# A two-layer decoder trunk on one core: slots ordered by the end of their last use, MLP activations stored in two steps, down operands gated by their loads

## The chip, the cores and the metric

The kernel runs on one core of one Trainium2 chip. The metric is the device time of one execution in microseconds; the figure for a kernel is the median of its runs. All arithmetic is on float32 values.

## What is computed

Two layers, each `h += post_norm(mixer(pre_norm(h)))` and then `h += post_norm(mlp(pre_norm(h)))`, on 1024 tokens by 1024 features. The mixers differ (gated MLP and pooling in layer 0, differential attention and a short convolution in layer 1). The change touches the MLP alone, which is the same in both layers:

```python
def squared_relu_mlp(h, w1, w2):                 # w1: 1024 x 4096, w2: 4096 x 1024
    return jnp.square(jax.nn.relu(h @ w1)) @ w2
```

## The kernel before

**Precision.** Every float32 operand is split in two parts: ScalarE casts a high part (`split_slot`, L624) and VectorE subtracts it for the low part (L625). A product is then three matmuls (`mm3`, L237 to L239: high by high, and the two cross terms).

**Tiling.** Each MLP matrix product is done by a 2 x 2 block scheme with seven products in place of eight. In the up half (`mlp_up`, L745) the 4096 hidden features go in 16 chunks `q`; a chunk has seven products of 12 matmuls (`plain` makes two, then `p6`, `p5`, `p7`, `p4`, `p3`). The first six chunks (`EARLY`) have done their two plain products ahead, so their iterations have five products. ScalarE copies partial sums out of PSUM (L753) and squares (L756, L757); VectorE forms sums of weights (`w1_sums`, L663 to L666) and of results. `sums(q)` (L824) forms the operands of the down half and issues four stores on the POOL queue: three pairs `x0`, `x1`, `x2` of 512 KB each (L838) and a half slot `u` of 256 KB (L839), all to the DRAM array `hs`. Eight units of the planner's clock later the four slots go back to the free list (L840).

The down half (`Down`, L1266) reads `hs` and `w2` again. Its 28 operand pairs are taken in the order of `ORDER`, four groups of seven. A product `n` is four quarters of 12 matmuls; the first four kinds of each group add up in the PSUM banks `pA`, the others in `pC`, and ScalarE copies the bank after each quarter in the first group (L1424), VectorE adds it to `acc` in the later ones (L1426). `prep(n)` takes the slots for product `n`, issues the load of the next activations (`load_h(n + 1)`) and some loads of weights on the SP queue (L614), and returns a list of steps: the two casts and subtractions of the activations (`hh`, `hl` from `hr`) first, then those of the weights (`wh`, `wl` from `w2r` or from a sum `t`). `step` runs the steps: two per quarter, or as many as are needed. It may begin `prep(n + 2)` while product `n` runs (`AHEAD = 2`), if 14 slots are free.

**Slots.** All of this lives in 50 slots of 4 KB per partition (`Slots`, L31). The free list is first in, first out. The planner's clock (`k.clock`) advances by the cost of each product (`pe`, 12 x 0.227 for a quarter or an up product) and says when `later` work is due. The order in the text is a priority: the framework then orders each engine's instructions by when it expects their operands, so an instruction can be put ahead of text that comes before it, and on the chip an engine runs its own list strictly in that order. A slot that is handed out again makes its new writer wait for all readers of the old content, a store among them.

Of the kernel before, what the change touches and what calls it, by code (L numbers as in the profile page):

```python
# [16 lines left out]
ALU = mybir.AluOpType  # L17
# [13 lines left out]
class Slots:  # L31


    def __init__(self, pool, n):
        self.pool = pool
        self.free = list(range(n))
        self.n = 0
        self.low = n
        self.live = {}

    def get(self, shape, dtype, name):
        if not self.free:
            raise RuntimeError(f"out of SBUF slots at {name}: {sorted(self.live.values())}")
        i = self.free.pop(0)
        self.low = min(self.low, len(self.free))
        self.n += 1
        self.live[i] = name
        t = self.pool.tile(shape, dtype, tag=f"s{i}", name=f"{name}_{self.n}")
        return Slot(self, i, t)


class Slot:
    def __init__(self, owner, i, t):
        self.owner, self.i, self.t = owner, i, t

    def put(self):
        self.owner.free.append(self.i)
        del self.owner.live[self.i]
        self.t = None


# [88 lines left out]
class Trunk:  # L150
    def __init__(self, ctx, tc, a):
        self.tc, self.nc, self.a = tc, tc.nc, a
        self.clock = 0.0
        self.q = []
        self.seq = 0
        self.small = ctx.enter_context(tc.tile_pool(name="small", bufs=1))
        self.tiny = ctx.enter_context(tc.tile_pool(name="tiny", bufs=5))
        self.slots = Slots(ctx.enter_context(tc.tile_pool(name="slots", bufs=1)), NSLOT)
        self.psp = ctx.enter_context(tc.tile_pool(name="psp", bufs=1, space=bass.MemoryType.PSUM))
        self.banks = list(range(8))  # L160
        dram = ctx.enter_context(tc.tile_pool(name="dram", bufs=1, space=bass.MemoryType.DRAM))
        self.hd = [dram.tile([S, DM], F32, name=f"hd{i}") for i in range(3)]
        self.ydd = dram.tile([2, 2, P, S], F32, name="ydd")
        self.skew = dram.tile([4, P * 384], F32, name="skew")
        self.W = Weights(self)
        self.ydone = {}
        self.xn = [[[None] * 4 for _ in range(2)] for _ in range(2)]
        self.xready = [[False, False], [False, False]]
        self.pend = {}
        self.xr = {}  # L170
        self.hs = [dram.tile([7, 4, P, 2048], F32, name=f"hs{i}") for i in range(2)]
# [573 lines left out]
    def mlp_up(self, layer):  # L745
        nc, sl = self.nc, self.slots
# [3 lines left out]
        Q = [dict() for _ in range(NQ)]  # L750
# [4 lines left out]
        def relu2(ap, src):  # L755
            nc.scalar.activation(ap, src, AF.Relu)  # L756
            nc.scalar.activation(ap, ap, AF.Square)  # L757
# [49 lines left out]
        def p4(q):  # L807
            d = Q[q]
            self.prod1(d["A"], q, "x", 0, "t4", False)
            self.w1q[q]["x"].put()  # L810
            relu2(d["x0"].t[:, 1, :], d["A"].t)
            d["A"].put()

        def p3(q):
            d = Q[q]
            self.prod1(d["C"], q, "sb", 1, "b22", False)
            for n in ("sb", "hsb"):
                self.w1q[q][n].put()
            c12 = d["x1"].t[:, 0, :]
            tt(c12, d["C"].t, d["u"].t[:, 1, :], op=ALU.add)  # L820
            d["C"].put()
            relu2(c12, c12)

        def sums(q):  # L824

            d = Q[q]
            g, r = q // 4, slice((q % 4) * 512, (q % 4) * 512 + 512)
            a11, a12 = d["x0"].t[:, 0, :], d["x0"].t[:, 1, :]
            a21, a22 = d["x1"].t[:, 0, :], d["x1"].t[:, 1, :]
            d["x2"] = sl.get([P, 2, 512], F32, "hx2")  # L830
            s1, s2 = d["x2"].t[:, 0, :], d["x2"].t[:, 1, :]
            tt(s1, a21, a22, op=ALU.add)
            tt(s2, s1, a11, op=ALU.subtract)
            tt(a21, a11, a21, op=ALU.subtract)
            tt(d["u"].t[:, 1, :], a12, s2, op=ALU.subtract)
            hs = self.hs[layer]
            for n, j in (("x0", 0), ("x1", 2), ("x2", 4)):
                nc.gpsimd.dma_start(hs[j:j + 2, g, :, r].rearrange("j p f -> p j f"), d[n].t)  # L838
            nc.gpsimd.dma_start(hs[6, g, :, r], d["u"].t[:, 1, :])  # L839
            self.later(8.0, lambda: [d[n].put() for n in ("x0", "x1", "x2", "u")])  # L840


        self.wait(lambda: self.xready[0] == [True, True])
# [30 lines left out]
        down = None  # L874
        for q in range(NQ):
            n = q + 1
            if n < NQ:
                if n > 1:
                    self.w1_sums(n)
                if n >= EARLY:  # L880
                    plain(n)
                if n > 1:
                    self.w1_split(n, "b")
                if n < EARLY:
                    p6(n)
                if self.HELD <= n + 1 < EARLY:
                    refill(n + 1)
                if q == 0:
                    next(xs)
            else:  # L890
                down.step(4, 0)
            p4(q)
            if n < NQ:
                self.w1_split(n, "a")
                if q == 0:
                    next(xs)
            else:
                down.step(8, 0)
            p3(q)
            if n < NQ:  # L900
                if n >= EARLY:
                    p6(n)
                if n + 2 < NQ:
                    if "raw" not in self.w1q[n + 2]:
                        self.w1q[n + 2]["raw"] = self.raw_w1(layer, n + 2)
                self.w1_a22(n)
                p5(n)
                sums(q)
                if n + 1 < NQ and n + 1 >= EARLY:
                    self.w1_plain(n + 1)  # L910
                p7(n)
                if n == NQ - 2:
                    down = Down(self, layer)
                    down.load_w(0, 11)
                    down.load_h(0)
                if n == NQ - 1:
                    down.load_h(1)
                    down.load_w(0, 22)
                    down.load_w(0, 12)
            else:  # L920
                sums(q)
# [344 lines left out]
class Down:  # L1266
# [10 lines left out]
    def __init__(self, k, layer):  # L1277
        self.k, self.layer = k, layer
        self.seq = [(g, i) for g in range(4) for i in self.ORDER]
        self.H, self.Wd, self.B, self.T = {}, {}, {}, {}  # L1280
        self.acc, self.banks = {}, {}
        self.todo = []
        self.ready = 0
        self.begun = 0

    def pair(self, name, dt=F32R):
        return [self.k.slots.get([P, 2, 512], dt, name) for _ in range(2)]

    def load_h(self, n):
        if n >= len(self.seq) or n in self.H:  # L1290
            return
        g, i = self.seq[n]
        self.H[n] = self.pair("hr", F32)
        for j in range(2):
            self.k.load(self.H[n][j].t.rearrange("p a b -> p (a b)"),
                        self.k.hs[self.layer][self.HJ[i], g, :, j * 1024:j * 1024 + 1024])

    def load_w(self, g, kn):

        if g > 3:  # L1300
            return
        self.B[g, kn] = self.pair("w2r", F32)
        b = (kn // 10 - 1) * 2 + kn % 10 - 1
        for j in range(2):
            self.k.load(self.B[g, kn][j].t.rearrange("p a b -> p (a b)"),
                        self.k.a["w2"][self.layer, g, b, :, j * 1024:j * 1024 + 1024])
# [19 lines left out]
    def prep(self, n):  # L1326
# [2 lines left out]
        T, B = self.T, self.B  # L1329
        hl = [self.pair("hh"), self.pair("hl")]  # L1330
        wl = [self.pair("wh"), self.pair("wl")]
        steps = self.split(hl, self.H.pop(n))
        self.load_h(n + 1)
        if i == 1:
            steps += self.split(wl, B[g, 11], True)
            T[3] = self.pair("t3", F32)
            steps += self.sub(T[3], B[g, 22], B[g, 12])
        elif i == 6:
            self.load_w(g, 21)
            T[2] = self.pair("t2", F32)  # L1340
            steps = self.tt(T[2], T[3], B[g, 11], ALU.add) + steps
            steps += self.split(wl, T[2], True)
        elif i == 7:
            steps += self.split(wl, T.pop(3))
# [12 lines left out]
            steps += self.split(wl, B.pop((g, 22 if i == 3 else 21)))  # L1357
            self.load_w(g + 1, 22 if i == 3 else 12)
        self.Wd[n] = (*hl, *wl)
        steps.append(self.one_ready)  # L1360
        return steps

    def one_ready(self):
        self.ready += 1

    AHEAD = 2

    def step(self, n, most):

        while n > 0:  # L1370
            if not self.todo:
                if (self.begun >= len(self.seq) or self.begun > most
                        or (self.begun > most - self.AHEAD + 1 and len(self.k.slots.free) < 14)):
                    return
                self.todo = self.prep(self.begun)
                self.begun += 1
            self.todo.pop(0)()
            n -= 1

    def finish(self, m):  # L1380
        while self.ready <= m:
            self.step(1, m)

    def run(self, hsrc, hdst):
        k, acc, seq = self.k, self.acc, self.seq
# [165 lines left out]
```

## Time and profile before

| | us |
|---|---|
| median of 3 runs | 1991.13 |
| lowest, highest run | 1985.10, 1991.89 |
| the profiled execution, its own time | 1989.53 |
| span from its first to its last instruction | 1987.7 |

TensorE (PE) is busy for nearly the whole span, so the time can only fall by the stretches in which PE waits or runs at a lower clock. In the tables of the trace "idle before" is the time an engine stood still ahead of an instruction, and the name behind the arrow is what ended it; `DMA hs<-hx` is the landing of a store of `x0`, `x1` or `x2`, `DMA hs<-u` that of `u`, `DMA hr<-hs` that of a load of activations.

### The profile page before, as it was taken

How to read it: one execution, taken by the hardware profiler on the slowest of the kernel's cores; microseconds unless marked ns; L12 is line 12 of the kernel's file. 1: busy time of each engine (PE TensorE's matmuls, PEld its weight loads, DVE VectorE, ACT ScalarE, POOL GpSimd, SP SyncE). 2: the span in 40 equal slices, each digit the busy share in tenths (PEclk: the TensorE clock that was granted, in tenths of full speed). 3: DMA queues.
4: the chain of work that ended last, by engine and by line, in shares of the span. 5: the costliest groups of instructions: out<-in, count | busy, mean ns of one | idle time of the engine just before them, and what ended most of it. 6: DMA issues, size and time to landing. Idle time of an engine off the chain costs nothing.

```text
span 1987.7 us, 23663 instructions
## 1 busy us (share of the span) xinstructions
PE 1948.4 (98%) x8840; PEld 1588.7 (80%) x8840; DVE 1278.4 (64%) x1979; ACT 982.9 (49%) x1632; POOL 208.5 (10%) x327
## 2 busy tenths in 40 slices
PE   9999999999999999999999999999999999999997
PEld 6888887788877888878778778788777888788886
DVE  5664496655577777683455556658665657767776
ACT  7223574555455443474344444657545545544342
POOL 3101101111110000031000001120111111000001
PEclk9999999999999999999999999999999999999999
DMA  8114226755675534452111103323565557544453
GB/s 296 42 61 131 85 97 189 181 148 148 181 211 183 176 108 161 161 187 82 43 43 43 32 33 106 117 96 106 162 185 151 154 160 226 181 146 160 150 177 130
DMA packets 77011, 269.84 MB, mean 136 GB/s; under 512 B 9221, under 2 KB 9221, under 8 KB 76896
## 3 DMA queue, kind: packets, MB, share of 16 engines
q1 hardware_dynamic: 48816, 170.94, 25.8%
q0 software_dynamic: 26784, 95.26, 16.4%
q10 hardware_dynamic: 1296, 2.13, 0.3%
q8 instruction: 69, 1.13, 0.2%
q14 instruction: 46, 0.38, 0.1%
HBM read 189.92 MB, written 78.38 MB: 135 GB/s over the span
## 4 chain that ended last, share of the span: by engine, by line
PE 59%; issue 29%; POOL 4%; DMA 3%; DVE 3%; ACT 1%; SPq 0%; POOLq 0%; DVEq 0%; ACTq 0%
PE pA L237 5%; PE pA L238 5%; PE pA L239 5%; PE pC L237 4%; PE pC L238 4%; PE pC L239 4%; POOL hs L838 3%; PE op L237 3%; PE op L239 3%; PE op L238 3%; PE pv L1226 1%; PE s L1159 1%; DMA hr<-hs 1%; DMA hs<-hx 1%; PE s L1162 1%
## 5 line engine op out<-in xcount | busy, mean ns | idle before, releaser
L624 ACT CAST hh<-hr 128x1024 fp32r<-128x1024 f32 x112 | 117.8, 1054 | 200.5 <-DMA hr<-hs 159.4
L237 PE MATMUL pA<-wh,hh 128*128 128x512 f32 x512 | 200.7, 392 | 8.0 <-ACT acc L1424 8.0
L238 PE MATMUL pA<-wl,hh 128*128 128x512 f32 x512 | 200.1, 391 | 0.8 <-DVE wl L625 0.8
L239 PE MATMUL pA<-wh,hl 128*128 128x512 f32 x512 | 200.0, 391 | 0.0
L625 DVE TENSOR_TENSOR hl<-hr,hh 128x1024 fp32r<-128x1024 f32 x112 | 136.2, 1222 | 89.9 <-ACT hh L624 86.7
L237 PE MATMUL pC<-wh,hh 128*128 128x512 f32 x384 | 150.1, 391 | 0.8 <-DVE acc L1426 0.8
L238 PE MATMUL pC<-wl,hh 128*128 128x512 f32 x384 | 149.7, 390 | 0.0
L239 PE MATMUL pC<-wh,hl 128*128 128x512 f32 x384 | 149.5, 389 | 0.0
L838 POOL DMA_DIRECT2D hs<-hx x96 | 69.3, 723 | 557.8 <-ACT hx L757 408.1
L237 PEld LDWEIGHTS pA<-wh,hh 128*128 128x128 f32 x512 | 96.5, 188 | 31.3 <-ACT acc L1424 11.0
L238 PEld LDWEIGHTS pA<-wl,hh 128*128 128x128 f32 x512 | 96.5, 188 | 21.4 <-DVE wl L625 1.4
L239 PEld LDWEIGHTS pA<-wh,hl 128*128 128x128 f32 x512 | 96.4, 188 | 19.9
L756 ACT ACTIVATE hx<-hx 128x512 f32<-128x512 f32 x96 | 60.7, 632 | 100.3 <-DVE hx L775 45.8
L114 DVE TENSOR_TENSOR wlo<-raw,whi 128x1024 fp32r<-128x1024 f32 (+1 forms) x57 | 68.3, 1203 | 48.4 <-ACT whi L113 31.1
L1426 DVE TENSOR_TENSOR acc<-acc,pA 128x512 f32<-128x512 f32 x96 | 65.2, 683 | 36.5 <-PE pA L239 36.5
L1195 ACT ACTIVATE e<-s,nm 128x512 f32<-128x512 f32 (+3 forms) x96 | 54.6, 579 | 63.7 <-DVE nm L1188 54.0
L237 PEld LDWEIGHTS pC<-wh,hh 128*128 128x128 f32 x384 | 72.3, 188 | 16.4 <-DVE acc L1426 1.2
L113 ACT CAST whi<-raw 128x1024 fp32r<-128x1024 f32 (+1 forms) x57 | 58.8, 1041 | 52.8 <-PE pp L239 15.8
L238 PEld LDWEIGHTS pC<-wl,hh 128*128 128x128 f32 x384 | 72.2, 188 | 14.9
L239 PEld LDWEIGHTS pC<-wh,hl 128*128 128x128 f32 x384 | 72.2, 188 | 14.9
L757 ACT ACTIVATE hx<-hx 128x512 f32<-128x512 f32 x128 | 81.1, 633 | 3.4
L625 DVE TENSOR_TENSOR wl<-w2r,wh 128x1024 fp32r<-128x1024 f32 x64 | 76.9, 1221 | 7.8 <-ACT wh L624 3.6
(332 smaller groups left out, 5156.3 us busy)
## 6 DMA issues: line engine op xcount, KB each, us to landing
hr<-hs SPq DMA_DIRECT2D x112, 512.0 KB, 5.3
hs<-hx POOLq DMA_DIRECT2D x96, 512.0 KB, 5.0
w1r<-in_w_dram SPq DMA_DIRECT2D x74, 512.0 KB, 4.3
w2r<-in_w_dram SPq DMA_DIRECT2D x64, 512.0 KB, 8.0
h<-hd POOLq DMA_DIRECT2D x24, 512.0 KB, 5.4
hs<-u POOLq DMA_DIRECT2D x32, 256.0 KB, 7.6
hd<-y POOLq DMA_DIRECT2D x12, 512.0 KB, 3.0
rx<-in_xT_dram SPq DMA_DIRECT2D x16, 256.0 KB, 7.4
```

The lines of the kernel that those rows point to most:

```text
L113: k.nc.scalar.copy(u.hi.t[:, f], u.raw.t[:, f])
L114: k.nc.vector.tensor_tensor(u.lo.t[:, f], u.raw.t[:, f], u.hi.t[:, f].bitcast(F32), op=ALU.subtract)
L237: mm(ps, ah, bh, start=start, stop=False, skip_group_check=more)
L238: mm(ps, ah, bl, start=False, stop=False, skip_group_check=more)
L239: mm(ps, al, bh, start=False, stop=stop, skip_group_check=more)
L624: self.nc.scalar.copy(hi, src)
L625: self.nc.vector.tensor_tensor(lo, src, hi.bitcast(F32), op=ALU.subtract)
L756: nc.scalar.activation(ap, src, AF.Relu)
L757: nc.scalar.activation(ap, ap, AF.Square)
L838: nc.gpsimd.dma_start(hs[j:j + 2, g, :, r].rearrange("j p f -> p j f"), d[n].t)
L1195: nc.scalar.activation(e[m][:, kb * 512:kb * 512 + n], banks[m, kb][:, :n], AF.Exp, scale=SCALE, bias=nm[:, m:m + 1], accum_out=sm[:, kb * ...
L1426: nc.vector.tensor_tensor(o, o, bank.t, op=ALU.add)
```

## The change

1. A slot that is put back carries a time, the planner's clock plus `after`; `get` takes the free slot with the lowest one. `after` is 6.0 for `x1`, `x2` and `u` at the end of `sums`, and 0 everywhere else.
2. The store of `x0` is issued at the end of `p4` and no longer in `sums`; the other three stay.
3. In `prep` the steps on the activations come last, behind those on the weights.
4. `step` begins the look-ahead `prep(n + 2)` only if at least 8.0 units of the planner's clock have gone by since the last load of the down half was issued.
5. In the last iteration of the up half the two calls `down.step(4, 0)` and `down.step(8, 0)` become `down.step(5, 1)` twice; `finish` calls `step` with a limit one higher.

```diff
     def get(self, shape, dtype, name):
-        i = self.free.pop(0)
+        i = min(self.free, key=lambda j: self.cool[j])
+        self.free.remove(i)
...
-    def put(self):
-        self.owner.free.append(self.i)
-        del self.owner.live[self.i]
+    def put(self, after=0.0):
+        o = self.owner
+        o.free.append(self.i)
+        o.cool[self.i] = o.k.clock + after
+        del o.live[self.i]
...
         def p4(q):
             relu2(d["x0"].t[:, 1, :], d["A"].t)
             d["A"].put()
+            store(q, 0, "x0")
...
+        def store(q, j, n):
+            r = slice((q % 4) * 512, (q % 4) * 512 + 512)
+            nc.gpsimd.dma_start(self.hs[layer][j:j + 2, q // 4, :, r].rearrange("j p f -> p j f"), Q[q][n].t)
...
-            for n, j in (("x0", 0), ("x1", 2), ("x2", 4)):
-                nc.gpsimd.dma_start(hs[j:j + 2, g, :, r].rearrange("j p f -> p j f"), d[n].t)
-            nc.gpsimd.dma_start(hs[6, g, :, r], d["u"].t[:, 1, :])
-            self.later(8.0, lambda: [d[n].put() for n in ("x0", "x1", "x2", "u")])
+            store(q, 2, "x1")
+            store(q, 4, "x2")
+            nc.gpsimd.dma_start(self.hs[layer][6, g, :, r], d["u"].t[:, 1, :])
+            self.later(8.0, lambda: [d[n].put(0.0 if n == "x0" else 6.0) for n in ("x0", "x1", "x2", "u")])
...
-                down.step(4, 0)
+                down.step(5, 1)
             p4(q)
...
-                down.step(8, 0)
+                down.step(5, 1)
             p3(q)
...
     def load_h(self, n):
         self.H[n] = self.pair("hr", F32)
+        self.loaded = self.k.clock
...
         self.B[g, kn] = self.pair("w2r", F32)
+        self.loaded = self.k.clock
...
-        steps = self.split(hl, self.H.pop(n))
+        steps, late = [], self.split(hl, self.H.pop(n))
         self.load_h(n + 1)
         if i == 1:
             steps += self.split(wl, B[g, 11], True)
+            steps, late = steps + late, []
...
-            steps = self.tt(T[2], T[3], B[g, 11], ALU.add) + steps
+            steps += self.tt(T[2], T[3], B[g, 11], ALU.add)
...
-        steps.append(self.one_ready)
-        return steps
+        return steps + late + [self.one_ready]
...
-    AHEAD = 2
+    AHEAD, LAND = 2, 8.0
...
                 if (self.begun >= len(self.seq) or self.begun > most
-                        or (self.begun > most - self.AHEAD + 1 and len(self.k.slots.free) < 14)):
+                        or (self.begun > most - self.AHEAD + 1
+                            and (len(self.k.slots.free) < 14 or self.k.clock - self.loaded < self.LAND))):
...
     def finish(self, m):
         while self.ready <= m:
-            self.step(1, m)
+            self.step(1, m + self.AHEAD - 1)
```

## Rows read from the trace of the kernel before

**Rows 1.** The page, busy time of each engine over the span, its share and its instructions.
```profile
PE 1948.4 (98%) x8840; PEld 1588.7 (80%) x8840; DVE 1278.4 (64%) x1979; ACT 982.9 (49%) x1632; POOL 208.5 (10%) x327
```

**Rows 2.** Busy time by stretch: up half of layer 0, start of its down half, the same two of layer 1. Columns: stretch and its length, then us busy and instructions of PE, PEld, DVE, ACT, POOL; granted clock of PE, share of the DMA engines' time, GB/s.
```profile
303.00:560.00 257.00, 252.63 (x1102) 207.12 (x1101) 156.24 (x209) 135.50 (x202) 38.25 (x56) 0.99 0.65 171
560.00:605.00 45.00, 38.60 (x163) 29.72 (x163) 32.16 (x33) 25.68 (x34) 4.75 (x7) 1.00 0.77 210
...
1360.00:1660.00 300.00, 294.75 (x1302) 242.18 (x1301) 193.68 (x250) 165.26 (x247) 39.46 (x58) 1.00 0.52 158
1660.00:1705.00 45.00, 41.84 (x173) 33.01 (x173) 34.15 (x35) 29.22 (x38) 4.75 (x7) 0.96 0.69 210
```

**Rows 3.** What PE waited for in the up half of layer 0 (303 to 560 us): us in total, times, longest.
```profile
PE pA L237 <- ACT u L753: 2.4, 2, 2.2
PE pA L239 <- DVE w1sb L625: 1.6, 1, 1.6
```

**Rows 4.** The same at the start of the down half of layer 0 (560 to 605 us).
```profile
PE pA L237 <- ACT acc L1424: 4.9, 4, 2.2
PE pC L237 <- DVE hx L804: 0.8, 1, 0.8
PE pA L238 <- DVE wl L625: 0.8, 1, 0.8
```

**Rows 5.** The same in the up half of layer 1 (1360 to 1660 us).
```profile
PE pA L237 <- ACT u L753: 3.5, 3, 1.8
PE pA L239 <- DVE w1sb L625: 1.3, 1, 1.3
```

**Rows 6.** The same at the start of the down half of layer 1 (1660 to 1705 us).
```profile
PE pA L237 <- ACT acc L1424: 3.2, 3, 2.0
```

**Rows 7.** The timeline of PE at five of these waits and one matmul behind the first: start, duration, instruction, and in brackets the idle time before it and what ended it.
```profile
339.18 0.50 PE L239 MATMUL pA<-xb,w1sb 128*128 128x512 f32 x1 [1.61 <-DVE w1sb L625]
339.52 0.39 PE L237 MATMUL pA<-xb,w1hsb 128*128 128x512 f32 x1
384.71 0.65 PE L237 MATMUL pA<-xb,w1hsa 128*128 128x512 f32 x1 [2.16 <-ACT u L753]
...
601.40 0.50 PE L237 MATMUL pA<-wh,hh 128*128 128x512 f32 x1 [2.16 <-ACT acc L1424]
...
1494.90 0.50 PE L237 MATMUL pA<-xb,w1x 128*128 128x512 f32 x1 [1.49 <-ACT u L753]
...
1697.88 0.50 PE L237 MATMUL pA<-wh,hh 128*128 128x512 f32 x1 [2.04 <-ACT acc L1424]
```

**Rows 8.** The timeline of DVE and ACT in the up half, instructions that waited for a store.
```profile
332.11 0.69 DVE L663 TENSOR_TENSOR w1va<-w1r 128x512 f32<-128x512 f32 x1 [5.26 <-DMA hs<-u]
...
377.14 1.23 DVE L625 TENSOR_TENSOR w1l<-w1r,w1h 128x1024 fp32r<-128x1024 f32 x1 [4.20 <-DMA hs<-u]
...
1432.67 0.69 DVE L663 TENSOR_TENSOR w1va<-w1r 128x512 f32<-128x512 f32 x1 [4.95 <-DMA hs<-u]
...
1477.38 1.22 DVE L625 TENSOR_TENSOR w1l<-w1r,w1h 128x1024 fp32r<-128x1024 f32 x1 [4.03 <-DMA hs<-u]
...
1492.37 1.05 ACT L624 CAST w1h<-w1r 128x1024 fp32r<-128x1024 f32 x1 [5.29 <-DMA hs<-hx]
```

**Rows 9.** Busy time by stretch, as in group 2, around the two stretches in which PE's clock was lower.
```profile
384.85:388.30 3.45, 3.45 (x9) 2.68 (x10) 1.73 (x3) 0.62 (x1) 2.02 (x3) 0.51 0.74 213
388.30:392.00 3.70, 3.70 (x18) 3.05 (x17) 1.79 (x2) 2.48 (x3) 0.00 (x0) 1.00 1.00 173
...
1699.00:1702.40 3.40, 3.40 (x10) 2.62 (x9) 1.39 (x2) 3.40 (x5) 0.00 (x0) 0.50 0.04 13
```

**Rows 10.** The timeline of ACT and POOL around one iteration of the up half: the last square of `x0`, the store of `x0`, the store of `u`.
```profile
330.07 0.63 ACT L757 ACTIVATE hx<-hx 128x512 f32<-128x512 f32 x1
331.00 0.71 POOL L838 DMA_DIRECT2D hs<-hx  x1 [6.67 <-ACT hx L757]
...
338.53 0.57 POOL L839 DMA_DIRECT2D hs<-u  x1
```

**Rows 11.** All DMAs that write or read `hs`, from issue to landing.
```profile
DMA to landing us min/median/max: 3.5/5.9/11.3
```

**Rows 12.** The timeline of ACT at the start of the down half of layer 0.
```profile
573.54 1.05 ACT L624 CAST wh<-t 128x1024 fp32r<-128x1024 f32 x1 [4.97 <-DMA hs<-u]
...
589.25 1.06 ACT L624 CAST hh<-hr 128x1024 fp32r<-128x1024 f32 x1 [6.74 <-DMA hr<-hs]
...
597.93 2.00 ACT L624 CAST hh<-hr 128x1024 fp32r<-128x1024 f32 x2 [1.75 <-DMA hr<-hs]
...
600.77 0.58 ACT L1424 COPY acc<-pA 128x512 f32<-128x512 f32 x1
...
621.26 1.05 ACT L624 CAST hh<-hr 128x1024 fp32r<-128x1024 f32 x1 [1.65 <-DMA hr<-hs]
```

**Rows 13.** The chain of work that ended last, at the same place: start, us, what.
```profile
583.01 10.03 DMA hs<-hx
593.05 4.79 DMA hr<-hs
```

**Rows 14.** One group of instructions on the tile `acc`: duration min/median/max, first and last start.
```profile
L1424 ACT COPY acc<-pC x24: 569/580/592, 645.9 to 1903.4; 128x512 f32<-128x512 f32 x24
```

**Rows 15.** Who waited for whom over the whole span: us in total, times, longest.
```profile
ACT hh L624 <- DMA hr<-hs: 159.4, 68, 13.4
DVE w1sb L625 <- PE pA L239: 33.7, 16, 3.6
```

**Rows 16.** DMA issues on the SP queue: count, size of one, median us from issue to landing.
```profile
hr<-hs SPq DMA_DIRECT2D x112, 512.0 KB, 5.3
w2r<-in_w_dram SPq DMA_DIRECT2D x64, 512.0 KB, 8.0
```

More of the change, by code (lines that the diff above doesn't have):

```diff
@@ L36, in __init__ @@
         self.free = list(range(n))
+        self.cool = [0.0] * n
+        self.k = None
         self.n = 0
@@ L158, in __init__ @@
         self.slots = Slots(ctx.enter_context(tc.tile_pool(name="slots", bufs=1)), NSLOT)
+        self.slots.k = self
         self.psp = ctx.enter_context(tc.tile_pool(name="psp", bufs=1, space=bass.MemoryType.PSUM))
@@ L835, in sums @@
             tt(d["u"].t[:, 1, :], a12, s2, op=ALU.subtract)
-            hs = self.hs[layer]
-            for n, j in (("x0", 0), ("x1", 2), ("x2", 4)):
-                nc.gpsimd.dma_start(hs[j:j + 2, g, :, r].rearrange("j p f -> p j f"), d[n].t)
-            nc.gpsimd.dma_start(hs[6, g, :, r], d["u"].t[:, 1, :])
-            self.later(8.0, lambda: [d[n].put() for n in ("x0", "x1", "x2", "u")])
+            store(q, 2, "x1")
+            store(q, 4, "x2")
+            nc.gpsimd.dma_start(self.hs[layer][6, g, :, r], d["u"].t[:, 1, :])
+            self.later(8.0, lambda: [d[n].put(0.0 if n == "x0" else 6.0) for n in ("x0", "x1", "x2", "u")])
         self.wait(lambda: self.xready[0] == [True, True])
@@ L1284, in __init__ @@
         self.begun = 0
+        self.loaded = 0.0
     def pair(self, name, dt=F32R):
```

## The prediction

> **What bounds the kernel now.** The page's busy times come first: PE works for 98% of the span, DVE for 64%, ACT for 49% [rows 1]. No change off PE can gain more than what PE loses to waits and to a lower clock. So the next view is busy time by stretch: in the four stretches of the MLPs that the change touches, PE stands still for 4.4, 6.4, 5.3 and 3.2 us (length less busy time) [rows 2]. The waits of PE in the same stretches say on whom. In both up halves it is ACT's copy of a partial sum and DVE's low part of the weights, 2.4 + 1.6 + 3.5 + 1.3 = 8.8 us in seven waits [rows 3, 5]; at both starts of the down half it is nearly always ACT's copy of the bank, 4.9 + 0.8 + 0.8 + 3.2 = 9.7 us in nine [rows 4, 6].
>
> The timeline says why ACT and DVE were late. In the up half the same engine had stood still some us earlier, ahead of an instruction whose slot still held data of a store in flight: DVE 5.26 us before w1va at 332, 4.20 before w1l at 377, ACT 5.29 before w1h at 1492 [rows 8]. About 7 us later PE stops at 339.18 and 384.71, and 2.5 us later at 1494.90 [rows 7]. At the start of the down half ACT stands 4.97 us for a store and 6.74 us for a load of activations [rows 12], and the chain shows where that load was held: a store landed after 10.03 us and only then the load ran, 4.79 us [rows 13]. The reader is to see that a store that lands late in a slot handed out early is what stops PE, two steps removed.
>
> Each stop costs more than its idle time. The step from matmul to matmul is 0.227 us (the code's own cost per matmul); a wait is counted from the modelled end, 0.39 us after the start, and the first step behind it takes 0.34 [rows 7]: 0.16 + 0.11 = 0.27 us on top. Two stops, of 2.16 and 2.04 us, were followed by 3.4 us at the granted clock 0.5, the 1.2 GHz level: 9 matmuls in 3.45 us, where the next stretch has 18 in 3.70 [rows 9], so 1.6 us lost each time.
>
> **The change, part by part.**
>
> Part 1, the order of slots. With `after` zero the lowest time is the slot put back first, as before; so all of it is that x1, x2 and u count as put back 6 units later. I stepped the free list through the code. From chunk 6 on, before, the chunk's hx2, w1h0 and w1l0 take the slots of x1, x2 and u, put back 10.9 units ago. With 6 units taken off they stand at 4.9 and fall behind w1x and w1va (8.2) and one w1sb (5.4), whose last reader is a PE product or a VectorE subtraction that is over. In the short iterations only two to seven slots are free; there w1va(4), which took u, takes a raw weight slot. So the five long waits of [rows 8] should go, with the stops behind them: of 8.8 us all but 0.4 (two of the short ACT waits), 8.4; five times 0.27, 1.4; one stretch at the lower clock, 1.6. **Up half: 11.4 us.**
>
> Is 6 units enough? A slot of q is then preferred from 14 units after `sums`. The stores are issued right behind `sums`, the last of them at 338.53 in the iteration shown, and land 3.5 to 11.3 us after their issue, median 5.9 [rows 10, 11]: 14 covers all. The Trainium skill (DMA: Bandwidth & Descriptors, Anatomy of one DMA) fits 2.0 us plus bytes over 436 GB/s for a DMA from this queue, an estimate of 3.2 us for 512 KB. By it the stores would land ahead of every reuse and this term would be nil; the trace's median is nearly twice that, and the measured waits decide.
>
> Part 2, the store of x0. POOL runs its list in order, and nothing stands between p4 and `sums` on it: the store of x0 is already issued as soon as the last square ends (330.07 + 0.63, issue at 331.00) [rows 10]. Four stores before, four after, the same waits: zero. What hides it is POOL's idleness; no more than the 0.3 us between square and issue can move.
>
> Part 3, activations last, and part 4, the gate. A load of activations is issued by the prep before the one that casts it. Two quarters of a product are 5.45 units, three are 8.17, so a gate of 8.0 makes a look-ahead prep start three quarters behind the last load and not two. Stepping `step` through both halves, this moves eight preps per layer (3, 6, 10, 13, 17, 20, 24, 27) by one quarter, 2.7 us; the reorder moves their casts by up to four steps, two quarters. Together the cast comes 2.7 to 8.2 us later, where ACT waits 159.4 / 68 = 2.3 us on average, 13.4 at most [rows 15]. Behind the cast on ACT stand the copies of the bank that PE waits for: that is the gain, and it counts only in the first group of a layer, where ACT empties the banks. With part 1 the load of activations for the fourth product takes x0's slot and a slot of the first product, no longer x1's, so it need not wait for the 10.03 us store. I count the largest stop of each layer, 2.16 + 2.04, two times 0.27 and the second stretch at the lower clock, 1.6: **start of the down half, 6.3 us.** The rest there, 5.5 us in seven waits and 1.9 for their restarts, 7.4 us, I leave as it is: ACT's 4.97 us at 573 [rows 12] is the cast of a product two ahead into u's slot, and since the reorder also puts the activation slots back later, my list gives that cast the same slot again. Bounds of this part: 0 and 13.7.
>
> What is queued behind the new waits: a prep that is held back delays its loads on SP and its casts on ACT and DVE. Cover: in layer 0 the cast at 621.26 is for a product whose first bank copy is at 645.9 [rows 12, 14], so some 20 us ahead of need.
>
> Part 5, the step budgets. The first prep has seven steps; 12 were allowed, now 10. The second is shut off as before, since the last loads are 0 and 2.7 units old at the two calls and 8 are asked. Zero. In `finish` the higher limit only keeps the gate from blocking a product that is due.
>
> New waits: slots that come later in the list are replaced by slots that PE has just let go, and a new order of the lists can put some instruction badly. The trace has no such wait in this place; the nearest row is DVE waiting for PE's reads, 33.7 / 16 = 2.1 us [rows 15]. Bounds: nothing, or four short iterations in two layers at 2.1, 16.8 us. I take two stops, one per layer, of about 2.1 plus restart: **4.5 us.**
>
> Sum: 11.4 + 6.3 - 4.5 = 13.2 us off the profiled execution's 1989.5 (its span is 1987.7), 1976.3. The median of the runs is 1.6 above the profiled one, so 1978 is the number to compare.
>
> **The rivals.**
>
> *The wait moves to PE's slots.* Writers of the short iterations now get slots released by the product just running, and PE stops for its own weights. For: few free slots there, and such waits exist. Against: most of them are 10 us ahead of use. At the upper bound 17.7 - 16.8 = 0.9 us remain: 1990.
>
> *Earlier loads collide with the last stores.* At the start of the down half the DMA engines are already 0.77 busy [rows 2], and a w2 load lands in 8.0 us where activations take 5.3 [rows 16]. If loads that start earlier lengthen the stores, the 6.3 is lost: 11.4 - 4.5 = 6.9, 1984. The Trainium skill (DMA: Bandwidth & Descriptors, Issuing engines are not separate DMA queues) says that all queues share the same 16 engines and interleave; no row here separates them.
>
> *All stops go.* 12.3 up (with the two small waits), 6.3 and 7.4 down: 26 us, 1965.
>
> *Slower: the gate eats the cover.* Place: the eight held preps of a layer; price a quarter, 2.7 us, each; it decides where a held prep's activations are cast after its product is due, that is when 8.2 us later is more than the lead. The lead of some 20 us speaks against it. If it decided in one layer: 6.9 - 21.8, that is 14.9 us slower, 2006.
>
> *The change does nothing,* because the framework's own ordering undoes it: 1991.
>
> **How the numbers follow.** My forecast 0.46, its own range 1973 to 1984 (charge of 0, half the up gain). Slots of PE 0.20, collision 0.12, all stops gone 0.12, slower 0.06, nothing 0.04. A measurement can tell about 0.5%, 10 us: below 1981 is faster, above 2001 slower. Faster: 0.36 of my forecast, 0.12 of all gone, 0.04 of the collision: 0.52. Slower: 0.06. Same: 0.42. The range reaches from 1966, beside the case of all stops gone, to 1990, which takes in collision and PE's slots.
>
> **What would show it.** Right: no DVE or ACT wait over 2 us on `hs<-u` or `hs<-hx` in the up half, no half-clock stretch near 385 and 1699, ACT's wait for `hr<-hs` well under 159 us, PE idle in the up halves under 2 us each. Part 2 is right if POOL's store of x0 still starts within 0.5 us of the square's end. Wrong: PE waits of the same length with another releaser (PE itself, or SP's loads), or PE's stops in the down half spread over all four groups, which would be the gate.

## The result and the profile after

| | before | after |
|---|---|---|
| median, us | 1991.51 (1985.10 to 1992.30, 4 runs) | 1970.49 (1969.81 to 1972.75, 4 runs) |
| the profiled execution: its time, its span, us | 1989.53, 1987.7 | 1972.75, 1970.8 |

The ratio is 0.9903, 95% interval 0.9881 to 0.9926: about 20 us off, where 13 were forecast. The two profiled executions differ by 16.9 us in span, and that is what can be read stage by stage.

PE's busy time fell by 5.6 us [rows 1]:

```profile
PE 1942.8 (99%) x8840; PEld 1587.9 (81%) x8840; DVE 1279.9 (65%) x1979; ACT 980.7 (50%) x1632; POOL 206.1 (10%) x327
```

The stages are cut at the same instructions in both kernels: at PE's first matmul with `w1hsb`, its last of the up half and its last of the down half, in each layer. So the lengths can be subtracted. Busy time by stretch, columns as in [rows 2]; the kernel before, then after:

```profile
285.91:568.50 282.59, 277.44 (x1210) 227.16 (x1208) 176.13 (x231) 150.78 (x224) 41.03 (x60) 0.99 0.62 164
568.50:887.77 319.27, 310.70 (x1370) 255.26 (x1369) 236.00 (x264) 159.18 (x207) 18.10 (x28) 0.99 0.50 168
1386.86:1667.90 281.04, 275.79 (x1210) 226.02 (x1208) 175.70 (x230) 149.94 (x223) 41.03 (x60) 1.00 0.55 166
1667.90:1976.88 308.98, 305.82 (x1339) 251.69 (x1337) 225.98 (x247) 140.97 (x175) 11.37 (x19) 0.99 0.49 163
```

```profile
284.80:566.01 281.21, 276.84 (x1210) 227.43 (x1208) 175.83 (x231) 149.53 (x224) 40.92 (x60) 0.99 0.64 166
566.01:875.97 309.96, 307.67 (x1370) 253.98 (x1369) 237.17 (x264) 160.01 (x207) 17.53 (x28) 1.00 0.51 172
1375.40:1657.19 281.79, 277.38 (x1210) 227.33 (x1209) 175.34 (x230) 148.94 (x224) 40.91 (x60) 0.99 0.55 167
1657.19:1960.24 303.05, 303.05 (x1339) 250.94 (x1337) 227.35 (x247) 141.08 (x175) 11.31 (x19) 1.00 0.50 165
```

The down halves give 9.3 and 5.9 us, 15.2 in all. The up halves, from which 11.4 was expected, give 1.4 and -0.8, 0.6 in all. A second profile of the changed kernel (below, under the runs that share a chip) has 281.2 and 279.6 us for them, without the stretch at the lower clock that the first has in layer 1: 2.9 us. So the up halves gave between 0.6 and 2.9 us, and the down halves are the same in both profiles within 0.4. What PE waited for in the up half of layer 0 (303 to 560 us), the start of its down half (560 to 605) and the up half of layer 1 (1340 to 1645); at the start of layer 1's down half it waited for nothing [rows 3 to 6]:

```profile
PE pC L245 <- DVE w1sa L631: 1.9, 1, 1.9
PE pA L243 <- ACT u L759: 1.8, 2, 1.6
PE pA L243 <- ACT w1h L630: 0.7, 1, 0.7
...
PE pA L243 <- ACT acc L1438: 1.5, 1, 1.5
...
PE pC L245 <- DVE w1sa L631: 1.8, 1, 1.8
PE pA L243 <- ACT u L759: 1.7, 2, 1.4
PE pA L243 <- ACT w1h L630: 0.7, 1, 0.7
PE pA L245 <- DVE w1sb L631: 0.2, 1, 0.2
```

The up halves have 8.8 us of PE's waits now, 5.1 of them under other names (`w1sa`, `w1h`). Before they had 10.4: the 8.8 of [rows 3, 5], two of 0.4 for `w1sa` that those rows leave out, and the 0.8 for `hx` in [rows 4], which lies at 565.87, before the up half's end. The starts of the down halves had 8.9 without that one, and have 1.5. Lines of after are 6 to 14 higher: the casts are L630, the subtraction of the low part L631, the copies of partial sums L759, of the bank L1438, the first sum of weights L669.

**Where the up half's waits went.** All waits of DVE and ACT for a store of the up half of layer 0 (285.9 to 568.5 us before, 284.8 to 566 after):

```profile
ACT w1h L624 <- DMA hs<-hx: 18.8, 7, 2.9
DVE w1l L625 <- DMA hs<-u: 10.3, 8, 4.2
ACT hh L624 <- DMA hs<-hx: 6.9, 1, 6.9
DVE w1va L663 <- DMA hs<-u: 5.3, 1, 5.3
DVE w1l L625 <- DMA hs<-hx: 4.0, 1, 4.0
ACT w1x L624 <- DMA hs<-hx: 3.4, 1, 3.4
ACT wh L624 <- DMA hs<-hx: 3.3, 1, 3.3
DVE w1vb L664 <- DMA hs<-u: 2.1, 1, 2.1
```

```profile
DVE w1va L669 <- DMA hs<-hx: 13.8, 7, 4.9
ACT wh L630 <- DMA hs<-hx: 10.5, 3, 9.3
ACT w1x L630 <- DMA hs<-hx: 2.1, 1, 2.1
DVE w1vb L670 <- DMA hs<-hx: 1.6, 1, 1.6
```

They fell from 54.1 to 28.0 us, and PE gained little. Three waits over 4 us are left, and PE's two largest stops stand behind two of them. The timeline of POOL and DVE around two of the long ones on `w1va`, then ACT's longest, with PE's stops behind the first and the last; the one at 375 reached no stop of PE:

```profile
301.10 0.69 DVE L669 TENSOR_TENSOR w1va<-w1r 128x512 f32<-128x512 f32 x1 [5.14 <-PE pC L244]
304.11 0.69 DVE L843 TENSOR_TENSOR hx<-hx 128x512 f32<-128x512 f32 x1
305.82 1.46 POOL L833 DMA_DIRECT2D hs<-hx  x2 [4.90 <-DVE hx L844]
314.42 0.69 DVE L669 TENSOR_TENSOR w1va<-w1r 128x512 f32<-128x512 f32 x1 [4.87 <-DMA hs<-hx]
318.23 0.50 PE L245 MATMUL pC<-xb,w1sa 128*128 128x512 f32 x1 [1.86 <-DVE w1sa L631]
...
366.67 1.45 POOL L833 DMA_DIRECT2D hs<-hx  x2 [4.96 <-DVE hx L844]
375.42 0.69 DVE L669 TENSOR_TENSOR w1va<-w1r 128x512 f32<-128x512 f32 x1 [4.38 <-DMA hs<-hx]
...
542.84 1.05 ACT L630 CAST wh<-w2r 128x1024 fp32r<-128x1024 f32 x1 [9.33 <-DMA hs<-hx]
545.37 0.50 PE L243 MATMUL pA<-xb,w1x 128*128 128x512 f32 x1 [1.61 <-ACT u L759]
```

DVE reached `w1va` at 314.42 - 4.87 = 309.55, that is 3.7 us after the issue of the stores of `x1` and `x2` began, and stood until one had landed, some 8 us behind its issue. PE's stop ended 3.8 us after that. Which slots are handed out can be stepped in the code. The next takers of the slots of `x1`, `x2` and `u`, in that order, and how many of the planner's units after these were put back (8 more since `sums`), in layer 0:

```text
                 before                6 units               12 units
chunk 0          w1x  x2   x1          w1va w1vb w1hsb       w1sb w1hsa w1sa
                 2.7  5.4  8.2         8.2  8.2  8.2         8.2  13.6  13.6
chunks 4 to 11   x2   w1h0 w1l0        w1va w1vb x0          w1vb x0    w1hsb
                 10.9 10.9 10.9        13.6 13.6 13.6        13.6 13.6  19.1
chunk 13         hh   hh   hl          wh   wh   wl          acc  acc   acc
                 13.6 13.6 13.6        13.6 13.6 13.6        19.1 19.1  19.1
chunk 15         hr   hh   hh          hr   hh   hh          hh   hl    hl
                 5.4  10.9 10.9        13.6 21.8 21.8        21.8 21.8  21.8
```

With 6 units the three slots are passed over for one product and then given to `w1va` and `w1vb`; those of chunk 13 go to the first `wh`, the cast that waits 9.33 us above. By the planner the `w1va` of chunk 0's row comes 16.2 units behind `sums`; on the chip DVE was there 3.7 us behind the stores that `sums` issues. DVE's list shows why, measured from the `w1va` of the chunk between (301.10): in the text it comes 2.7 units behind `sums`, on the chip 3.0 us ahead of `sums`' first sum (304.11); and the next `w1va` comes 13.6 units behind it in the text, on the chip 8.5 us (309.55). So against that instruction `sums` is 5.7 us late and the next `w1va` some 5 us early.

Two stops, the 1.86 us at 318.23 and in layer 1 one of 1.43 us at 1416.38 on ACT's copy of `u`, were also followed by stretches at the 1.2 GHz level; the stretches of [rows 9] are gone. Stretch, columns as there:

```profile
318.80:322.15 3.35, 3.35 (x9) 2.67 (x8) 1.47 (x3) 2.47 (x4) 0.71 (x1) 0.50 0.86 300
1417.85:1421.25 3.40, 3.40 (x8) 2.67 (x9) 3.39 (x5) 1.26 (x2) 0.00 (x0) 0.50 0.60 121
```

**Where the down half's gain came from.** What the SP queue waited for on stores of `x0` to `x2` between 535 and 625 us, before and after (total, times, longest):

```profile
SPq L614 <- DMA hs<-hx: 25.2, 3, 11.5
```

```profile
SPq L620 <- DMA hs<-hx: 19.1, 3, 7.5
```

ACT at the start of the down half of layer 0 [rows 12], and its wait for activations over the whole span [rows 15]:

```profile
568.14 1.05 ACT L630 CAST wh<-t 128x1024 fp32r<-128x1024 f32 x1 [3.36 <-DMA hs<-u]
...
582.73 1.05 ACT L630 CAST hh<-hr 128x1024 fp32r<-128x1024 f32 x1 [4.67 <-DMA hs<-hx]
...
591.28 1.06 ACT L630 CAST hh<-hr 128x1024 fp32r<-128x1024 f32 x1 [2.13 <-DMA hr<-hs]
```

```profile
ACT hh L630 <- DMA hr<-hs: 124.1, 65, 5.8
```

The longest single wait for activations fell from 13.4 to 5.8 us. The last chunk's `x1` used to go to a load of activations 5.4 units after it came back, and now after 13.6. That load is a part of the gain and not all of it, as the runs by chunk show below.

### The profile page after: what moved, and what is told of

Its sections match the earlier page's. It is cut to its first block, busy times and chain, and to the rows that moved or that the text cites. A ratio compares the mean times of both kernels' runs of the same rounds, so it can differ in the third digit from the quotient of the medians.

```text
span 1970.8 us, 23611 instructions
## 1 busy us (share of the span) xinstructions
PE 1942.8 (99%) x8840; PEld 1587.9 (81%) x8840; DVE 1279.9 (65%) x1979; ACT 980.7 (50%) x1632; POOL 206.1 (10%) x327
## 4 chain that ended last, share of the span: by engine, by line
PE 70%; issue 19%; DVE 4%; POOL 3%; ACT 2%; DMA 2%; SPq 0%; POOLq 0%; DVEq 0%; ACTq 0%
PE pA L245 8%; PE pA L243 8%; PE pA L244 7%; PE pC L245 4%; PE pC L244 4%; PE pC L243 4%; PE op L243 3%; PE op L245 3%; PE op L244 3%; POOL hs L833 1%; PE pv L1236 1%; PE s L1169 1%; PE s L1172 1%; ACT junk L260 1%; PE bg L243 1%
## 5 line engine op out<-in xcount | busy, mean ns | idle before, releaser
L630 ACT CAST hh<-hr 128x1024 fp32r<-128x1024 f32 x112 | 117.6, 1052 | 154.1 <-DMA hr<-hs 124.1
L631 DVE TENSOR_TENSOR hl<-hr,hh 128x1024 fp32r<-128x1024 f32 x112 | 136.0, 1221 | 60.6 <-ACT hh L630 56.0
L630 ACT CAST wh<-w2r 128x1024 fp32r<-128x1024 f32 x64 | 66.8, 1052 | 57.1 <-PE pA L244 26.3
L762 ACT ACTIVATE hx<-hx 128x512 f32<-128x512 f32 x96 | 60.3, 628 | 65.1 <-DVE hx L827 45.1
L631 DVE TENSOR_TENSOR wl<-w2r,wh 128x1024 fp32r<-128x1024 f32 x64 | 78.0, 1222 | 15.3 <-ACT wh L630 14.2
```

The costliest lines, as they stand in the source:

```text
L630: self.nc.scalar.copy(hi, src)
L631: self.nc.vector.tensor_tensor(lo, src, hi.bitcast(F32), op=ALU.subtract)
```

## The experiments

The theory taken into them: the up half's gain is nil because waits of the same length replaced the old ones; the down half's comes from parts 3 and 4, and the order of slots is worth little. The rival: the order of slots frees the loads of the down half, and carries most of the gain. Where nothing else is said the edit is to the changed kernel, and the ratio is to the kernel before on the same chip.

**The order of slots undone.**

```diff
-            self.later(8.0, lambda: [d[n].put(0.0 if n == "x0" else 6.0) for n in ("x0", "x1", "x2", "u")])
+            self.later(8.0, lambda: [d[n].put(0.0) for n in ("x0", "x1", "x2", "u")])
```

> The changed kernel with the 6 units for x1, x2 and u set to 0, so slots come back in order of their release, as before. Theory (the up halves gained next to nothing, 0.6 us over both layers, and the 15.2 us came in the down halves, from casts that come later): 1970 to 1975, the down halves as short as in the changed kernel (310 and 303 us), the up halves as before (282.6 and 281.0). Rival (slots whose stores are still in flight held the loads of the down half, so the order made its gain): 1979 or more, the down halves back by 5 us or more.

Measured 1988.62 us (1983.86 to 1993.19, 12 runs), ratio 0.9989 [0.9975, 1.0002]. The theory fell: with everything but this, nearly all of the gain is gone. PE waits at the start of both down halves as before (560 to 605, 1650 to 1705 us), and the SP queue waits for the stores as before:

```profile
PE pA L243 <- ACT acc L1438: 4.4, 3, 2.5
PE pA L244 <- DVE wl L631: 0.8, 1, 0.8
...
PE pA L243 <- ACT acc L1438: 3.6, 3, 2.1
...
SPq L620 <- DMA hs<-hx: 25.5, 3, 11.3
```

**The order of slots alone, on the kernel before.** The edit is part 1 of the change and no more.

> The kernel before with part 1 alone: slots by time, 6 units on x1, x2 and u; stores, steps, gate and budgets as before. Theory (the order made 18 us of the changed kernel's gain, the reorder of steps and the gate another 3 to 7): 1976 to 1982. Rival (the order frees the loads only when the casts also come later, so it is worth nothing alone): 1988 to 1993.

Measured 1977.87 us (1974.61 to 1978.81, 6 runs) against 1990.56, ratio 0.9932 [0.9916, 0.9949]: 12.7 us. The theory held: part 1 alone carries most of the gain; the rest needs the other parts on top of it, since without part 1 they are worth nearly nothing.

**The store of `x0` back in `sums`.**

```diff
             d["A"].put()
-            store(q, 0, "x0")
...
             tt(d["u"].t[:, 1, :], a12, s2, op=ALU.subtract)
+            store(q, 0, "x0")
```

> The changed kernel with the store of x0 issued in sums again. Theory (POOL issues it right behind the last square in any case, so the move is worth nothing): 1970 to 1973, every stage within 1 us. Rival (the moved store changes the order that the framework gives to the instructions around it): a stage differs by more than 2 us, in either direction.

Measured 1972.17 us (1971.01 to 1972.95, 6 runs), ratio 0.9905 [0.9888, 0.9923]. Part 2 is worth nothing that can be told. By stage it is within 0.5 us of the changed kernel's second profile.

**The activations first again.**

```diff
-        steps, late = [], self.split(hl, self.H.pop(n))
+        steps, late = self.split(hl, self.H.pop(n)), []
...
-            steps += self.tt(T[2], T[3], B[g, 11], ALU.add)
+            steps = self.tt(T[2], T[3], B[g, 11], ALU.add) + steps
```

> The changed kernel with the steps on the activations first again. Theory (part 3 and the gate together keep ACT from standing for loads ahead of its bank copies): half of the down gain is lost, 1976 to 1981, with PE waits on the bank copies at the starts of the down halves again. Rival (the order of slots did it alone): 1970 to 1973.

Measured 1977.63 us (1973.08 to 1979.25, 6 runs), ratio 0.9930 [0.9912, 0.9947]: the part is worth 0.0027 of the time, 5 us, on top of the others. Against the kernel with only the store moved back, timed on the same chip, it is 5.5 us, and no run of one lies among those of the other. The profile, the fastest of its six runs, shows some 2 us of this in layer 0's down half. Most of that lies where the prediction did not look, at its end, where the norm needs the last result. ACT, then PE:

```profile
834.69 1.05 ACT L630 CAST hh<-hr 128x1024 fp32r<-128x1024 f32 x1 [9.83 <-DMA hr<-hs]
...
860.96 1.31 PE L296 MATMUL tp<-ident,x 128*128 128x128 f32 x10 [1.81 <-ACT x L272]
```

The kernel before has the same pair, 10.81 us at 844.57 and 1.85 at 869.16; the changed kernel has neither. Where the other 3 us of the slower runs lie no profile shows.

**The gate off.**

```diff
-    AHEAD, LAND = 2, 8.0
+    AHEAD, LAND = 2, 0.0
```

> The changed kernel without the gate (0 in place of 8 units). Theory: the look-ahead preps come a quarter earlier, ACT waits for loads again in front of the bank copies, 1974 to 1979. Rival (eight held preps per layer with some 20 us of lead change nothing that PE sees): 1970 to 1972.

Measured 1973.35 us (1970.90 to 1977.12, 6 runs), ratio 0.9912 [0.9895, 0.9929]: between the two bands and within the interval of the changed kernel. The edit does one thing more than the text above it says: with part 5's limit and no gate, the second prep of each layer begins in the up half, 5.4 units earlier than in the kernel before. The profile, the slowest of the six, has three stops of PE on the bank copies in layer 1's down half, 2.5 us in all, where the changed kernel has none. The gate's worth is 0 to 3 us; what of it belongs to the eight held preps is not settled.

**Which chunks matter.** Six units for some chunks only, zero for the rest: chunks 14 and 15, chunks 0 to 13, chunks 13 to 15.

```diff
-            self.later(8.0, lambda: [d[n].put(0.0 if n == "x0" else 6.0) for n in ("x0", "x1", "x2", "u")])
+            self.later(8.0, lambda: [d[n].put(0.0 if n == "x0" or q < 14 else 6.0) for n in ("x0", "x1", "x2", "u")])
```

(`q >= 14` in the second, `q < 13` in the third.)

> The changed kernel with the 6 units only for the slots of the last two up chunks (14 and 15), the ones whose stores are in flight when the down half takes its first slots. Theory (the order gains in the down half, by those slots): 1970 to 1974, down halves 310 and 303 us, up halves with the old waits on the stores of u. Rival (the order of slots in the earlier chunks carries through): 1984 or more.

> The changed kernel with the 6 units only for chunks 0 to 13. Theory: the down halves are slow again as with no units at all, 1985 to 1990, the up halves as in the changed kernel. Rival: 1970 to 1974.

> The changed kernel with the 6 units for chunks 13 to 15 alone. Theory (the first prep of the down half takes the slots of chunk 13, so the down gain needs three chunks and not two): 1971 to 1975, down halves within 1.5 us of the changed kernel's, up halves with the old waits on the stores of u. Rival (what chunks 0 to 12 do to the order of the free list is needed too): 1977 or more.

Measured 1980.46 us (1979.16 to 1982.69), ratio 0.9950 [0.9934, 0.9967]; 1977.66 (1976.36 to 1979.69), 0.9934 [0.9916, 0.9952]; 1972.86 (1970.44 to 1975.26), 0.9915 [0.9901, 0.9929], 6 runs each. By the ratios, against 0.9989 with the order undone, the last two chunks give 0.0039 of the time or 7.8 us, the first fourteen 11, the last three 14.7, and all of them 17. My expectation that two chunks suffice fell, and so did the one that chunks 0 to 13 leave the down halves slow; the third held. Three chunks do nearly all, and chunk 13, added to the last two, is worth 7. Its slots go to operands of the down half either way; with six units to those of weights, with zero to those of activations (table above). With zero for chunks 14 and 15 the last chunk's `x1` goes to the load of activations at 5.4 units again, and the SP queue waits 24.9 us for stores between 535 and 625 us, as much as in the kernel before; yet the down halves are 313.2 and 304.0 us. So the load behind `x1` is not the only path.

**Twelve units in place of six.**

```diff
-            self.later(8.0, lambda: [d[n].put(0.0 if n == "x0" else 6.0) for n in ("x0", "x1", "x2", "u")])
+            self.later(8.0, lambda: [d[n].put(0.0 if n == "x0" else 12.0) for n in ("x0", "x1", "x2", "u")])
```

> The changed kernel with 12 units in place of 6. Theory (6 units only moved the wait in the up half from the slots of u to w1va on those of x1 and x2; longer keeps those slots out for another product): waits on stores in the up half fall below a third of the changed kernel's, its PE stops of 1.9 and 1.8 us with the half clock behind them go, 1962 to 1968. Rival (too few slots are free, so a later order puts the writers on slots that PE is still reading): 1971 to 1978.

Measured 1974.83 us (1972.27 to 1981.92, 6 runs), ratio 0.9925 [0.9905, 0.9946]: the time is in the rival's band, and of the theory the part on the up half held. The waits on stores in layer 0's up half fell to 8.9 us, none over 2.4, but its down half grew from 310.0 to 316.4 us, in a profile that is the slowest of the six runs, with two stretches of 6.8 us at 1.2 GHz in this MLP. ACT's wait there is for a store and not, as the rival had it, for PE's reads. ACT, then PE, in this kernel:

```profile
593.14 1.99 ACT L630 CAST hh<-hr 128x1024 fp32r<-128x1024 f32 x2 [10.30 <-DMA hs<-hx]
...
595.66 0.79 PE L243 MATMUL pA<-wh,hh 128*128 128x512 f32 x1 [5.16 <-ACT acc L1438]
```

**Twelve units for chunks 0 to 11, six for the rest.**

```diff
-            self.later(8.0, lambda: [d[n].put(0.0 if n == "x0" else 6.0) for n in ("x0", "x1", "x2", "u")])
+            self.later(8.0, lambda: [d[n].put(0.0 if n == "x0" else 12.0 if q < 12 else 6.0) for n in ("x0", "x1", "x2", "u")])
```

> The changed kernel with 12 units for chunks 0 to 11 and 6 for chunks 12 to 15. Theory (12 units take the stores' waits out of the up half, where the run with 12 everywhere had 278 us in layer 1, but put the first loads of the down half on slots that come too late): both up halves 276 to 279 us, down halves 310 and 303 as in the changed kernel, 1963 to 1967. Rival (what the up half gains, the start of the down half loses, since it begins with other slots): 1969 to 1975.

Measured 1965.32 us (1964.09 to 1965.56, 4 runs), ratio 0.9878 [0.9863, 0.9892]. It and the changed kernel were then timed on one chip:

> The changed kernel again, so that it and the next run share a chip and the runs of the kernel before. Earlier, on different chips, its ratio to before was 0.9903 [0.9881, 0.9926], that of the version with 12 units for chunks 0 to 11 and 6 for the rest 0.9878 [0.9863, 0.9892]: the intervals overlap. My theory (12 units take away most waits on stores in the up halves, 2.4 and 5.1 us by the profiles, nothing else changes): this kernel 3 to 8 us above the next one. Rival (what differed were the chips and the number of stretches at the lower clock): within 2 us of each other.

> 12 units for chunks 0 to 11 and 6 for the rest, on the same chip as the run before this one. My theory: 3 to 8 us under it, up halves of 277 to 279 us against 281 to 282. Rival: within 2 us of it.

Measured 1972.10 us (1969.28 to 1973.69, 5 runs), ratio 0.9905 [0.9891, 0.9919], for the changed kernel, and 1967.44 (1964.49 to 1969.26, 4 runs), 0.9880 [0.9866, 0.9894], for this version: 4.7 us less, the slowest run of one just under the fastest of the other. Busy time by stage in this version:

```profile
283.90:562.42 278.52, 275.44 (x1209) 226.11 (x1208) 176.75 (x231) 149.73 (x224) 40.93 (x60) 1.00 0.65 167
562.42:872.73 310.31, 307.48 (x1371) 253.99 (x1369) 237.25 (x264) 159.60 (x207) 16.82 (x28) 1.00 0.52 172
1372.16:1648.85 276.69, 275.12 (x1210) 226.22 (x1208) 176.21 (x230) 149.85 (x224) 40.90 (x60) 1.00 0.57 170
1648.85:1951.90 303.05, 303.05 (x1339) 250.94 (x1337) 227.52 (x247) 141.41 (x175) 11.32 (x19) 1.00 0.49 165
```

The up halves are 278.5 and 276.7 us, where the changed kernel has 281.2 and 281.8 above, and 281.2 and 279.6 in its second profile. The down halves keep their gain. That is the up half's gain that the change aimed at and missed: 5.5 to 7.8 us, of which 5.5 is between two profiles without a lower clock in the up halves. The 9.2 us wait of `wh` for chunk 13's store stays, with a stop of PE of 1.51 us behind it.

**The stages in these runs.** Lengths in us, cut at the same instructions as above, one profile each; in brackets the number of 3.4 us stretches at 1.2 GHz in the stage:

| | up, layer 0 | down, layer 0 | up, layer 1 | down, layer 1 |
|---|---|---|---|---|
| before | 282.6 (1) | 319.3 (1) | 281.0 | 309.0 (1) |
| after | 281.2 (1) | 310.0 | 281.8 (1) | 303.1 |
| after, second profile | 281.2 | 309.6 | 279.6 | 303.1 |
| order of slots undone | 282.5 (1) | 315.9 (1) | 281.4 (1) | 309.7 (1) |
| order of slots alone | 281.1 | 316.8 (3) | 280.1 | 303.1 |
| activations first again | 281.1 | 312.0 | 279.4 | 303.2 |
| six units for chunks 14, 15 | 283.6 (1) | 313.2 | 281.1 (1) | 306.0 |
| six units for chunks 0 to 13 | 281.5 (1) | 313.2 | 279.6 | 304.0 |
| six units for chunks 13 to 15 | 281.9 (1) | 309.7 | 281.6 | 303.1 |

In layer 1 the down half's gain is part 1's: whole with part 1 alone, none with all but part 1. In layer 0 the parts need each other: part 1 alone gives 2.4 us and all the others 3.4, together they give 9.3. The last stage with all but part 1, then with part 1 alone, columns as in [rows 2]:

```profile
1667.15:1976.83 309.68, 305.83 (x1339) 251.85 (x1337) 228.23 (x247) 141.39 (x175) 11.32 (x19) 0.99 0.49 162
1662.58:1965.66 303.08, 303.08 (x1338) 250.93 (x1337) 225.43 (x247) 140.45 (x175) 11.33 (x19) 1.00 0.49 165
```

## Why the prediction was right in the sum and wrong in its terms

The forecast was 1978.0 us and the median is 1970.5. By the profiles 13.2 us were forecast and 16.9 measured. Two terms were far off and stood on opposite sides; that their errors nearly cancel is luck, and the sum says little for the working.

**Up half: 11.4 forecast, 6.9 with the new waits taken off, 0.6 measured (2.9 by the second profile).** The step that failed is "So the five long waits of [rows 8] should go, with the stops behind them", and under it "14 covers all". In after `w1l` and `w1h` wait for no store, and no wait of the up half for `u` is over 0.2 us. But the slots went one product later to `w1va` and `w1vb`, on the same in-order engine. I followed who stops taking the three slots and not who takes them next. And 14 units were counted on the planner's clock from `sums`, where the chip counts from POOL's issue to DVE's arrival: 3.7 us, against a landing of 8. The runs with twelve units test this by itself: `w1va` of the short iterations and of the chunks behind them gets other slots, its long waits and PE's stops on `w1sa` are gone, and with six units kept for the last four chunks both up halves are shorter.

**Restarts and the lower clock in the up half: 1.4 + 1.6 forecast.** In the first profile nothing of it came, since the number of stops hardly fell, and layer 1 got a stretch at 1.2 GHz that it had not had; in the second no up half has such a stretch, so 1.6 of it came there. Layer 1's sum in the first profile closes on this alone: idle time 5.25 to 4.41, 0.8 less, one stretch of 1.6 more, 0.8 us longer.

**Start of the down half: 6.3 forecast, 15.2 measured for the whole down half.** The mechanism was right in part: with part 1 the load of activations no longer takes `x1`'s slot early, and the 11.5 us wait of the queue became 7.5. What I did not step are the slots of chunk 13, worth 7 us by the runs. The size was off in two ways. I counted the largest stop of each layer and left 5.5 us and their restarts standing; in fact 7.4 of the 8.9 us went. And the stops at the end of layer 0's down half (2.2 us, of which 0.7 stayed; 1.85 of them behind a 10.81 us wait for activations, with one more stretch at the lower clock) and one of 0.8 us at 629.70 lie behind the last of my rows, at 605 us. In layer 0 idle time fell from 319.27 - 310.70 = 8.6 to 2.3 us, five stops fewer (eight, now three) at 0.27 make 1.4, the stretch 1.6: 9.3, as measured. In layer 1 it is 3.2 + 0.8 + 1.6 = 5.6, where 5.9 was measured.

**"My list gives that cast the same slot again"** held: ACT still waits for `u` at 568.14, 3.36 us. No stop of PE follows it for 25 us; the one that then comes, 1.48 us at 593.81, has it on the chain behind it. So it cost PE 1.5 us at most, and leaving all the rest of the stops standing on its account was wrong.

**New waits: 4.5 charged.** Two new stops of 1.9 and 1.8 us, one per layer, did come, the size and number that I took; but from stores in flight, not from slots that PE had just let go. They stand in the up half's 0.6 already.

**Parts 2 and 5: zero.** Part 2 held, by the run that undoes it. Part 5 was not tried alone.

**Parts 3 and 4.** I put the down half's gain on the casts' order and the gate, with part 1 as a help. The runs turn that round: 17 us go with the order of slots, 5 to 7 with the order of steps, 0 to 3 with the gate (and with the second prep that it holds). The terms overlap, so they don't add to the whole.

**The rivals.** PE's own slots did not stop it: ACT's casts into `w1hsa` wait for PE's reads more than before (18.9 us in eight waits in layer 0's up half, 2.6 in two before), but no stop of PE names `w1hsa`. The collision did not come: the down halves gained most, and a `w2` load lands in 7.4 us (median) where it took 8.0. That all stops go was nearly right for the down halves alone: none is left in layer 1, three in layer 0. The gate cost nothing: without it the time is higher if anything.

**The signs set out beforehand.** Three held: ACT's wait for `hr<-hs` fell from 159 to 124 us, no lower clock is left near 385 and 1699, and POOL's store of `x0` starts 0.3 us behind the square's end (334.37 behind 333.45 + 0.63). Two did not: waits of up to 9.3 us on stores are left in the up halves, and PE is idle 4.4 us in each.

**A rule beside the rows.** In the trace of after the store that `w1va` waited for landed some 8 us after its issue. The Trainium skill (DMA: Bandwidth & Descriptors, Anatomy of one DMA) gives an estimate of 3.2 us for 512 KB on this queue; by it DVE, which came 3.7 us behind the first of the two issues and 3.0 behind the second, would have waited 0.2 us. The trace does not agree.

## What to carry to other kernels

When an order of slots is changed, follow each slot to its next writer and the one after: a store in flight does not stop costing when its slot is passed over once, it stops the next in-order engine that gets it. A hold time has to be measured from the store's issue to the writer's arrival on the chip, not on the clock of the program text. And the hold that serves one stage (twelve units in the up half) can hurt the next (six at its end), so choose it by stage.

## What the runs showed of the hardware that was not expected

A stop of 1.4 to 2.2 us on PE is sometimes followed by some 3.4 us at the 1.2 GHz level and sometimes not, in two executions of one kernel: the changed kernel's first profile has such a stretch at 318.8, behind the stop of 1.86 us at 318.23; its second has 1.73 us at the same instruction, at 316.94, and none behind it. The kernel with the order of slots alone stops for 1.87 us at 1415.89 and stays at 2.4 GHz. Each costs about 1.6 us, and a stage that no edit touches shows it: between the MLPs of the two layers the profiles of all these kernels take 499.1 to 499.4 us with no such stretch (5 profiles), 500.4 to 501.0 with one (5), 502.5 to 502.6 with two (4). Over the 48 runs of the kernel before that were timed beside these kernels, the mean granted clock goes with the time: 1992.4 to 1995.7 us at 0.992 (5 runs), 1984.7 to 1988.7 at 0.997 (4 runs), with a correlation of -0.79. So a large part of the 10 us between runs of one program goes with these stretches, as far as the clock tells, and two single profiles differ by several us in stages that the edit did not touch.
